# Output channels dealt over the SBUF partitions of a sparse 3x3 convolution, in a pattern of 16 x 8

## Chip, cores, metric

One core of one Trainium2 chip. The metric is device time in microseconds (us) of one execution. A page of the profile shows one profiled execution, whose span from first to last instruction is some 2 us shorter than the time. A run over 1.5% above the fastest of its kernel counts as slow, and ratios leave it out. "Row" below is one partition's contiguous piece of a DMA, here 16 KB of one output channel.

## The reference

```python
batch, c_in, h, w, c_out, k = 16, 64, 64, 64, 128, 3      # x: 16x64x64x64 f32, weight: 128x64x3x3 f32
x_pad = np.pad(x, ((0, 0), (0, 0), (1, 1), (1, 1)))
for b, co, ci, kh, kw:                                      # cut: five nested loops
    output[b, co] += weight[co, ci, kh, kw] * x_pad[b, ci, kh:kh+h, kw:kw+w]
```

x is 16.8 MB, the output 33.6 MB. The weights are 90% zeros, which the kernel does not use.

## The kernel before

Two images lie side by side on the 128 input partitions. TensorE makes the nine taps as matmuls; nearly everywhere it works on pairs of rows, whose input rows GpSimd has added up first. ScalarE (ACT) and VectorE (DVE) bring the sums from PSUM (the matmuls' output memory) to `o`, in SBUF (the on-chip memory that the DMA engines read): one tile of 128 channels x 64 x 64 per image, channel c on partition c. Stores of the first two pairs of images are held back until the loads are nearly done.

```python
    w_sb = const_pool.tile([C_OUT, C_IN * KH * KW], FP32, name="w_sb")
    nc.sync.dma_start(out=w_sb, in_=weight.rearrange("o i kh kw -> o (i kh kw)"))
    x_head = o_pool.tile([128, H, W], FP32, name="o")
    nc.sync.dma_start(out=x_head[:, 0:HEAD, :], in_=pair(0)[:, 0:HEAD, :])        # x's first half, cast later
    nc.gpsimd.dma_start(out=xs[0][:, HEAD:H, :], in_=pair(0)[:, HEAD:H, :])       # its second half, cast by the DMA
    ident = const_pool.tile([128, 128], BF16, name="ident")
    make_identity(nc, ident)
    for p in range(1, NP):
        nc.gpsimd.dma_start(out=xs[p], in_=pair(p))
    # ... cut: casts and transposes of the weights, matmuls, evictions ...
    HELD = 2
    held = []

    def store(p, n, o, a, b):
        return nc.sync.dma_start(out=out[2 * p + n][:, a:b, :], in_=o[n][:, a:b, :])

    for p in range(NP):
        o = [o_pool.tile([C_OUT, H, W], FP32, name="o") for _ in range(2)]
        # ... cut: four blocks of rows; at p == HELD, after the first block, the held stores go out,
        #     the first of them behind a wait for that block's last eviction ("loads first");
        #     the last pair is stored in two halves of rows, all others whole ...
```

Of the kernel before, what the change touches and what calls it, by code (L numbers as in the profile page):

```python
# [27 lines left out]
def kernel(  # L28
# [6 lines left out]
    nc = tc.nc  # L35
# [21 lines left out]

    xs = [x_pool.tile([128, H, W], BF16, name=f"x{p}") for p in range(NP)]
    w_sb = const_pool.tile([C_OUT, C_IN * KH * KW], FP32, name="w_sb")
    nc.sync.dma_start(out=w_sb, in_=weight.rearrange("o i kh kw -> o (i kh kw)"))  # L60
    x_head = o_pool.tile([128, H, W], FP32, name="o")
    nc.sync.dma_start(out=x_head[:, 0:HEAD, :], in_=pair(0)[:, 0:HEAD, :])
    nc.gpsimd.dma_start(out=xs[0][:, HEAD:H, :], in_=pair(0)[:, HEAD:H, :])  # L63
# [112 lines left out]
    held = []  # L176

    def store(p, n, o, a, b):
        return nc.sync.dma_start(out=out[2 * p + n][:, a:b, :], in_=o[n][:, a:b, :])

    for p in range(NP):
        o = [o_pool.tile([C_OUT, H, W], FP32, name="o") for _ in range(2)]
        last = p == NP - 1
        for blk in range(4):
            r0 = 16 * blk
            if BLOCKS[p][blk] == "T":
                done = twos(p, o, r0)
            else:
                for r, rows in ((r0, 8), (r0 + 8, 8)):
                    direct(p, o, r, rows)  # L190
            if last and blk % 2 == 1:
                for n in range(2):
                    store(p, n, o, r0 - 16, r0 + 16)
            if p == HELD and blk == 0:
                first = store(*held[0])
                tc.add_manual_dep(
                    first.ins,
                    done.ins.name,
                    mybir.DependencyInfo(
                        mybir.DependencyClass.Sync, mybir.DependencyReason.DATA  # L200
                    ),
                    reason="loads first",
                )
                for args in held[1:]:
                    store(*args)
        if p < HELD:
            held += [(p, n, o, 0, H) for n in range(2)]
        elif not last:
            for n in range(2):
                store(p, n, o, 0, H)  # L210
# [30 lines left out]
```

## Time and profile before

| | kernel before |
|---|---|
| time | 128.09 us (127.72 to 129.0, 4 runs beside the changed kernel) |
| span of the profiled run | 125.6 us |
| store of 2 MB, issue to landing, median | 17.0 us |
| 16 KB store row on its engine, mean (median) | 615 ns (611 ns) |

### The profile page before, as it was taken

To read this page: it belongs to the slowest core of one execution; us is meant where nothing else is said; L and a number is where in the kernel's file an instruction comes from. 1 tells how busy PE (TensorE), PEld (TensorE's weight loads), DVE (VectorE), ACT (ScalarE), POOL (GpSimd) and SP (SyncE) were. 2 spreads that over 40 slices of the span, in tenths; PEclk is the share of its full clock that TensorE was granted. 3 is DMA by queue.
4 is the path that set the end of the run, shared out by engine and by line. 5 is a ranking of instruction groups with operands and counts; after the bars stand their busy time and mean duration, and the time that the engine had idled before them with its cause. 6 is when DMAs were issued, how large, how long until landed. Compare 5 with 4: busy or idle time off the path is not lost.

```text
span 125.6 us, 2486 instructions
## 1 busy us (share of the span) xinstructions
PE 108.9 (87%) x1002; PEld 57.2 (46%) x1002; DVE 82.3 (66%) x135; ACT 38.9 (31%) x71; POOL 40.7 (32%) x45
## 2 busy tenths in 40 slices
PE   6669999999999999999999999999999999960000
PEld 6424455555555555545555555555555555420000
DVE  0352577877787778777877878887888787770000
ACT  4541533333333333333333333333333333320000
POOL 6937333333333333333333333333333310000000
PEclk9999999999999999999999999999999999999555
DMA  4999999999999999999999999999999999999960
GB/s 126 353 223 224 214 209 214 211 224 217 217 209 214 318 425 433 438 428 420 423 433 428 438 428 417 428 433 420 443 428 417 417 417 428 428 410 412 425 269 10
DMA packets 4044, 42.93 MB, mean 342 GB/s; under 512 B 448, under 2 KB 448, under 8 KB 704
## 3 DMA queue, kind: packets, MB, share of 16 engines
q1 hardware_dynamic: 2880, 34.90, 66.0%
q0 software_dynamic: 1152, 7.86, 30.2%
q8 instruction: 8, 0.13, 0.4%
q14 instruction: 4, 0.03, 0.1%
HBM read 17.07 MB, written 33.55 MB: 403 GB/s over the span
## 4 chain that ended last, share of the span: by engine, by line
PE 82%; DMA 4%; DVE 1%; issue 1%; DVEq 0%; SPq 0%
PE ps L135 82%; DMA o<-in_x_dram 4%; DVE o L168 1%; DVEq L236 0%; DVE x L87 0%; SPq L60 0%; DVEq L168 0%
## 5 line engine op out<-in xcount | busy, mean ns | idle before, releaser
L168 DVE TENSOR_TENSOR o<-ps,pc 128x512 f32<-128x512 f32 x124 | 77.8, 686 | 22.1 <-PE ps L135 19.8
L135 PE MATMUL ps<-x,wT 64*128 64x504 bf16 (+3 forms) x780 | 90.0, 377 | 1.8 <-DVE x L87 1.8
L135 PEld LDWEIGHTS <-wT 64*128 64x128 bf16 x966 | 53.6, 95 | 52.6 <-issue 3.3
L154 POOL TENSOR_TENSOR s<-x 128x512 bf16<-128x512 bf16 x31 | 35.6, 1152 | 59.3 <-PE ps L135 43.1
L161 ACT COPY pc<-ps 128x512 f32<-128x512 f32 x62 | 33.3, 589 | 64.0 <-issue 61.8
L135 PE MATMUL ps<-s,wT 64*128 64x512 bf16 (+1 forms) x186 | 25.6, 377 | 0.0
L74 PE MATMUL ps<-idle_rhs 128*128 128x128 bf16 x27 | 3.1, 313 | 1.0 <-DVE idle_rhs L71 1.0
L67 POOL DMA_DIRECT2D x<-in_x_dram x7 | 3.7, 561 | 0.0
L149 DVE COPY o<-ps 128x512 f32<-128x512 f32 x2 | 1.4, 692 | 3.3 <-PE ps L135 3.3
L74 PEld LDWEIGHTS <-idle_rhs 128*128 128x128 bf16 x27 | 2.8, 148 | 1.0 <-DVE idle_rhs L71 1.0
L91 DVE CAST w_bf<-w_sb 128x192 bf16<-128x192 f32 (+1 forms) x4 | 1.1, 349 | 2.8 <-DMA w_sb<-in_weight_dram 2.8
L148 ACT COPY o<-ps 128x512 f32<-128x512 f32 x2 | 1.2, 586 | 3.7 <-PE ps L135 3.7
L87 ACT CAST x<-o 128x576 bf16<-128x576 f32 (+1 forms) x2 | 1.5, 802 | 0.8 <-DMA o<-in_x_dram 0.8
L87 DVE CAST x<-o 128x576 bf16<-128x576 f32 x1 | 0.5, 461 | 1.9 <-DMA o<-in_x_dram 1.9
L91 ACT ACT_TABLE_LOAD x1 | 1.3, 1283 | 0.7 <-PEq L225 0.7
L97 PE MATMUL ps<-ident,w_bf 128*128 128x128 bf16 x9 | 1.2, 308 | 0.3 <-DVE w_bf L91 0.3
L91 ACT CAST w_bf<-w_sb 128x64 bf16<-128x64 f32 (+1 forms) x2 | 0.7, 416 | 1.7 <-DMA w_sb<-in_weight_dram 1.7
L97 PEld LDWEIGHTS <-w_bf 128*128 128x128 bf16 x9 | 0.8, 129 | 0.7 <-DVE w_bf L91 0.7
L101 DVE TENSOR_TENSOR wT<-ps,wT 128x384 bf16<-128x384 f32 x2 | 1.0, 548 | 0.0
L63 POOL DMA_DIRECT2D x<-in_x_dram x1 | 0.7, 696 | 0.8 <-POOLq L225 0.8
L71 DVE MEMSET idle_rhs<- 128x64 uint32 x1 | 0.1, 112 | 0.8 <-PEq L225 0.8
L110 ACT CAST wT<-ps 128x384 bf16<-128x384 f32 x1 | 0.5, 478 | 0.3 <-PE ps L97 0.3
(8 smaller groups left out, 1.9 us busy)
## 6 DMA issues: line engine op xcount, KB each, us to landing
out_dram<-o SPq DMA_DIRECT2D x14, 2048.0 KB, 17.0
x<-in_x_dram POOLq DMA_DIRECT2D x7, 1024.0 KB, 25.1
out_dram<-o SPq DMA_DIRECT2D x4, 1024.0 KB, 11.0
o<-in_x_dram SPq DMA_DIRECT2D x1, 1024.0 KB, 5.6
x<-in_x_dram POOLq DMA_DIRECT2D x1, 512.0 KB, 7.5
w_sb<-in_weight_dram SPq DMA_DIRECT2D x1, 288.0 KB, 3.0
```

Of the source, the lines that this page charges most:

```text
L67: nc.gpsimd.dma_start(out=xs[p], in_=pair(p))
L74: nc.tensor.matmul(idle_ps, idle_rhs, idle_rhs, start=True, stop=True)
L87: copy(out=xs[0][:, a:b, :], in_=x_head[:, a:b, :])
L91: copy(out=w_bf4[:, g, a:b, :], in_=w_v[:, k : k + b - a, :])
L97: nc.tensor.matmul(wps[:, j, :], src, ident, start=True, stop=True)
L101: nc.vector.tensor_tensor(out=wT[:, g], in0=wps, in1=wT[:, G1], op=SUB)
L135: nc.tensor.matmul(ps[n][:, lo:hi, c_lo:c_hi], tap(g, kw, n), src[q, a:b:step, c_lo + kw - 1 : c_hi + kw - 1], start=(i == 0), stop=(i == ...
L148: nc.scalar.copy(out=o[0][:, r0 : r0 + rows, :], in_=ps[0])
L149: nc.vector.tensor_copy(out=o[1][:, r0 : r0 + rows, :], in_=ps[1])
L154: nc.gpsimd.tensor_tensor(out=s, in0=xs[p][:, r0 : r0 + 16 : 2, :], in1=xs[p][:, r0 + 1 : r0 + 16 : 2, :], op=ADD)
L161: nc.scalar.copy(out=c, in_=shared[n])
L168: done = nc.vector.tensor_tensor(out=o[n][:, first : r0 + 16 : 2, :], in0=ps[n], in1=pc[n], op=ADD)
```

## The change

Its intent: what the 16 engines write at one moment should be sixteen neighbouring channels, 256 KB in one piece. Which channels an engine writes at which moment, no trace shows. Nothing in the computation changes; the weights are loaded in the same permuted order in which the channels are stored.

```diff
-    nc.sync.dma_start(out=w_sb, in_=weight.rearrange("o i kh kw -> o (i kh kw)"))
+    nc.sync.dma_start(
+        out=w_sb,
+        in_=weight.rearrange("(a b) i kh kw -> b a (i kh kw)", b=16),
+    )
...
     def store(p, n, o, a, b):
-        return nc.sync.dma_start(out=out[2 * p + n][:, a:b, :], in_=o[n][:, a:b, :])
+        dst = out[2 * p + n].rearrange("(a b) h w -> b a h w", b=16)
+        return nc.sync.dma_start(out=dst[:, :, a:b, :], in_=o[n][:, a:b, :])
```

## The prediction

The recorded text is cut, and the cuts are marked, where it told of the hardware what no run here shows. With them go terms of its sum: the cost of a clash in the stores (0 to +69 us, some 30 as a middle) and 0.7 us for the weight load. The sum came to 127.6 to 128.9 us without a clash and to 132 to 198 with one; the point was 134 us, and the range ended at 182. By a clash it means store rows up to twice as long as their floor of 611 ns, by a lead how far one engine is ahead of another.

> **What bounds the kernel now.** I read the page's row of slices first, then its queues, then the engines by stretches of time, then the chain that ended last with the list of DMA issues, and last the packet records and landings in the trace.
>
> ```profile
> PE   6669999999999999999999999999999999960000
> ...
> DMA  4999999999999999999999999999999999999960
> GB/s 126 353 223 224 214 209 214 211 224 217 217 209 214 318 425 433 438 428 420 423 433 428 438 428 417 428 433 420 443 428 417 417 417 428 428 410 412 425 269 10
> ...
> q1 hardware_dynamic: 2880, 34.90, 66.0%
> q0 software_dynamic: 1152, 7.86, 30.2%
> ...
> HBM read 17.07 MB, written 33.55 MB: 403 GB/s over the span
> ```
>
> Two rows are full: PE from the fourth slice to the 36th, DMA from the second to the 38th (a slice is 125.6/40 = 3.14 us). The GB/s row looks half empty up to slice 13, but there the loads cast to bf16 and the row counts the 7.86 MB they write, half of what they read. So the DMA engines have no slack in either half: x in the first, stores in the second.
>
> ```profile
> core 0: us, PE busy (x) PEld busy (x) DVE busy (x) ACT busy (x) POOL busy (x), PEclk, DMA share, GB/s
> ...
> 60.00:80.00 20.00, 20.00 (x192) 10.35 (x190) 15.93 (x27) 6.44 (x12) 6.91 (x6) 1.00 1.00 427
> 80.00:100.00 20.00, 20.00 (x190) 10.32 (x188) 15.79 (x27) 6.59 (x13) 6.97 (x7) 1.00 1.01 427
> 100.00:113.30 13.30, 11.94 (x112) 5.95 (x108) 10.53 (x17) 4.14 (x8) 1.10 (x1) 1.00 1.00 419
> 113.30:125.60 12.30, 0.00 (x0) 0.00 (x0) 0.00 (x1) 0.00 (x0) 0.00 (x0) 0.60 0.66 277
> ```
>
> PE and DMA are full side by side; after 113.3 us only DMA works.
>
> ```profile
> PE ps L135 82%; DMA o<-in_x_dram 4%; DVE o L168 1%; DVEq L236 0%; DVE x L87 0%; SPq L60 0%; DVEq L168 0%
> ...
> out_dram<-o SPq DMA_DIRECT2D x14, 2048.0 KB, 17.0
> ...
> out_dram<-o SPq DMA_DIRECT2D x4, 1024.0 KB, 11.0
> ```
>
> The chain names PE, but its shares add up to some 90%; the rest is the last stores, which it does not follow. A 2 MB store takes 17 us to land where its bytes at 427 GB/s need 4.9: it waits behind two or three others. The landings of the last store (two halves' worth issued at 113.3) come between 120.9 us on the first engine and 124.4 on the last. From 113.3 to 120.9 is 7.6 us of work, of which the last two 1 MB stores are 2.1 MB / 427 GB/s = 4.9; so 2.7 us of backlog were there when PE had finished. The store queue never ran dry: **the DMA rate sets the end**, and PE follows at most 2.7 us behind.
>
> The sum agrees. One engine's share is 8 rows of every transfer. A 16 KB store row takes 611 ns in 88% of the packet records (mean 617), a half row 313, a cast load row 625. Stores: 14 x 8 x 0.617 + 4 x 8 x 0.313 = 79.1 us. Loads: 7 x 8 x 0.625 + 16 x 0.313 + weights 0.8 = 40.8. With the first packet at 1.7 us that makes 121.6; the last packet ends at 124.0. The store rate, 16 x 16384 B / 611 ns = 429 GB/s, is a floor repeated to the nanosecond, not a mean over stalls.
>
> [...]
>
> **The change part by part.**
> - *Compute*: partition p holds channel 16(p mod 8) + p div 8 from the weight load to the store. Transposes, matmuls, evictions keep their shapes and counts. Cost 0.
> - *Packets*: each row stays one contiguous run (2304 B, 8 or 16 KB) on both sides. 20 hardware DMAs, the same 2560 data packets. Issue cost: 386 ns median on SP, maybe more for a pattern with one dimension more, but SP waits 99 us for DVE in total. Cost 0.
> - *HBM side*: [...] A better locality can save only what is above the floor: (617 - 611)/611 = 1% of 79 us = 0.8 us. It may do nothing.
> - *SBUF side*: [...] The leads: in the last x load, before the stores take over, nine of 16 engines landed within 0.43 us (0.7 of a row), the last 2.9 us later (4.7 rows); in the stores near the end the spread is 3.6 us. So leads are small at first and wander by single stalls (0.3 to 0.9 us). [...]
> - *Weight load*: [...]
>
> Sum: without a clash 128.4 - 0.8 to + 0.5 us; with one, some 132 to 198 us, middle near 160, since nothing hides a slower store.
>
> **The rivals.**
> 1. *Nothing changes* (about 128.4 us)[...]
> 2. [...]
> 3. *A better balance* (down to 126 us): the last engine lands 3.5 us after the first and 2.5 us after the mean of the 16 (121.9). If its lag came from the addresses it always writes, dealing the channels would spread it. Against: the lag is there in the x loads too (1 us, then 2.9) and grows in steps; between 15 and 113 us there are eight 16 KB instruction fetches beside it, which stay.
> 4. *PE becomes the bound*: only if stores sped up by over 2.7 us; they cannot at the floor.
>
> **Range and chances.** I give the clash a little over half (0.52)[...]. No visible change 0.42, a gain over 2% (2.6 us, the whole skew) 0.06. The mixture has its middle at about 134 us, between its two humps and itself not a favourite: under it lies all of rivals 1 and 3, above it the clash. The tenth part lies under 127.2 us[...].
>
> **What would show it.** The length of 16 KB store rows decides: 611 ns still in nine tenths of them means no clash; lengths up to 1222 ns, a GB/s row of 220 to 380 in the second half and a full PE row with gaps (DVE waiting for o buffers that are not yet stored) mean the clash. If rows stay at 611 and the end moves, the spread of the last landings must have moved with it. The weight load's 3.0 us to landing should grow by under 1 us. The prediction is wrong in its reasons if rows stay at 611 and the time still differs by over 2%, or if rows lengthen evenly on all engines [...].

## The result, and the profile after

The changed kernel takes 142.25 us (141.1 to 144.69, 4 runs, of which the longest counts as slow) against 128.09. The ratio is 1.106, 95% interval 1.094 to 1.118. Ratios here and below are the mean time of one kernel's fast runs over that of the other's in the same rounds, so not quite the ratio of the medians quoted. The span of the profiled run went from 125.6 to 139.2 us.

The rows by slices of the changed kernel (one slice is now 3.48 us):

```profile
PE   7309999999999999999949999999999999200000
...
DMA  4999999999996999999999999999999999999840
GB/s 99 287 273 221 219 217 212 214 219 212 214 219 129 226 257 264 287 306 351 377 409 414 414 433 424 424 421 428 428 428 409 438 414 419 381 318 377 341 181 28
```

But for the 13th slice, where loads give way to stores, DMA is as full as before. Yet from the 14th slice on it moves 226 to 287 GB/s where the kernel before soon moved 420. The rate then climbs for some 25 us, reaches the old 425, and falls again near the end. Busy engines at half the rate means rows that take longer. The engines by stretches of time say the same, one line of the kernel before and then three of the changed one:

```profile
41.00:60.00 19.00, 19.00 (x182) 9.73 (x179) 14.77 (x24) 6.44 (x12) 6.93 (x6) 1.00 1.01 413
```

```profile
core 0: us, PE busy (x) PEld busy (x) DVE busy (x) ACT busy (x) POOL busy (x), PEclk, DMA share, GB/s
...
41.00:60.00 19.00, 19.00 (x182) 9.46 (x178) 14.80 (x25) 6.45 (x12) 6.92 (x6) 1.00 0.93 232
60.00:80.00 20.00, 18.06 (x154) 8.77 (x152) 12.63 (x21) 5.37 (x10) 5.77 (x5) 0.91 1.00 384
80.00:100.00 20.00, 20.00 (x191) 10.55 (x189) 15.90 (x27) 6.45 (x12) 6.91 (x6) 1.00 1.01 426
```

Between 60 and 80 us PE, too, has a gap. The waits and the chain name it: DVE waits for `o` buffers that are not stored yet (before it had no such wait), and the chain now runs through a store.

```profile
DVE o L172 <- DMA out_dram<-o: 4.6, 2, 3.9
```

```profile
PE ps L139 57%; DMA out_dram<-o 17%; DMA o<-in_x_dram 6%; SPq L184 2%; DVE o L172 2%; SPq L61 0%; DVEq L241 0%; DVE x L91 0%; DVEq L172 0%
...
out_dram<-o SPq DMA_DIRECT2D x14, 2048.0 KB, 22.7
...
out_dram<-o SPq DMA_DIRECT2D x4, 1024.0 KB, 17.3
o<-in_x_dram SPq DMA_DIRECT2D x1, 1024.0 KB, 8.3
...
w_sb<-in_weight_dram SPq DMA_DIRECT2D x1, 288.0 KB, 3.6
```

The last two lines show a second thing: x's first half lands 8.3 us after its issue. In the kernel before they read:

```profile
o<-in_x_dram SPq DMA_DIRECT2D x1, 1024.0 KB, 5.6
...
w_sb<-in_weight_dram SPq DMA_DIRECT2D x1, 288.0 KB, 3.0
```

The start by time, SP's and GpSimd's issues and the first matmul on x, before:

```profile
0.74 0.38 SPq L60 DMA_DIRECT2D w_sb<-in_weight_dram  x1
...
1.17 0.43 SPq L62 DMA_DIRECT2D o<-in_x_dram  x1
1.24 0.70 POOL L63 DMA_DIRECT2D x<-in_x_dram  x1 [0.79 <-POOLq L225]
...
7.36 5.29 PE L135 MATMUL ps<-x,wT 64*128 64x512 bf16 x36 [1.83 <-DVE x L87]
```

and after:

```profile
0.74 0.66 SPq L61 DMA_DIRECT2D w_sb<-in_weight_dram  x1
...
1.24 0.70 POOL L67 DMA_DIRECT2D x<-in_x_dram  x1 [0.79 <-POOLq L230]
1.46 0.56 SPq L66 DMA_DIRECT2D o<-in_x_dram  x1
...
10.34 5.74 PE L139 MATMUL ps<-x,wT 64*128 64x512 bf16 x36 [4.47 <-DVE x L91]
```

The weight load with its extra dimension takes 0.66 instead of 0.38 us to issue, so the load of x's first half is issued after GpSimd's load of the second half, not before. In the packet records the consequence is plain. Between 4.5 and 5.0 us the engines of the kernel before start 26 rows of the first half and none of the second. Those of the changed kernel start 12 of the first and 14 of the second. The half that is needed first shares the engines with the one that is needed later, and the first matmul on x starts 3.0 us later.

From the packet records, the mean length of the 16 KB store rows that start in stretches of 8 us (without the eight instruction fetches of the same size, which the prediction's row mean of 617 ns includes; all these tables come from one profiled run of each kernel):

| ns | 43-51 us | 51-59 | 59-67 | 67-75 | all |
|---|---|---|---|---|---|
| before | 617 | 615 | 614 | 615 | 615 |
| after | 1138 | 971 | 768 | 651 | 697 |

And from the landings of each store on the 16 engines, the time between the first engine's and the last engine's, for the first five stores in order: changed kernel 1.3, 3.2, 5.3, 6.6, 7.0 us; it stays between 7.0 and 7.5 up to the 13th. Before: 2.5, 2.5, 2.5, 2.3, 2.3.

The records carry no engine numbers, but on a busy engine a row starts within some 20 ns of the end of the one before it, so the rows can be strung into chains, one for each engine, with some doubt where two ends coincide. In the changed kernel 31 of the 32 rows that are second and third in the 16 chains take 1204 to 1406 ns. Soon many chains repeat every four rows, as one does with 611, 611, 864, 1496, 611, 611, 613, 1496 ns. Of the rows over 900 ns that start between 50 and 66 us, 64% are followed by another such row four rows later, and 21% two rows later (43% of all rows there are so long).

Now the 13.6 us between the spans (the last landing moved from 124.5 to 138.1) can be put together, per engine in the mean of the 16: whole store rows 112 x (697 - 615) ns = 9.2 us, half rows 32 x (345 - 313) ns = 1.0 us, the later start 2.0 us (not measured by itself, but what is left of the 12.2 us by which the mean landing of the last store moved; the first store row starts 2.4 us later, at 44.3 us), and 1.5 us because the last engine now lands 4.1 us after the mean, before 2.6.

### The profile page after: what moved, and what is told of

Same layout as the page of the kernel before. It is cut to its first block, busy times and chain, and to the rows that moved or that the text cites. A ratio compares the mean times of both kernels' runs of the same rounds, so it can differ in the third digit from the quotient of the medians.

```text
span 139.2 us, 2486 instructions
## 1 busy us (share of the span) xinstructions
PE 110.9 (80%) x1002; PEld 57.2 (41%) x1002; DVE 82.2 (59%) x135; ACT 39.0 (28%) x71; POOL 40.8 (29%) x45
## 4 chain that ended last, share of the span: by engine, by line
PE 57%; DMA 23%; SPq 3%; DVE 2%; issue 1%; DVEq 0%
PE ps L139 57%; DMA out_dram<-o 17%; DMA o<-in_x_dram 6%; SPq L184 2%; DVE o L172 2%; SPq L61 0%; DVEq L241 0%; DVE x L91 0%; DVEq L172 0%
## 5 line engine op out<-in xcount | busy, mean ns | idle before, releaser
L139 PE MATMUL ps<-x,wT 64*128 64x504 bf16 (+3 forms) x780 | 94.5, 382 | 6.4 <-DVE x L91 4.5
L139 PE MATMUL ps<-s,wT 64*128 64x512 bf16 (+1 forms) x186 | 28.9, 385 | 0.0
L116 DVE CAST wT<-ps 128x384 bf16<-128x384 f32 x1 | 0.6, 551 | 0.0
```

Source lines behind the costliest of these rows:

```text
L139: nc.tensor.matmul(ps[n][:, lo:hi, c_lo:c_hi], tap(g, kw, n), src[q, a:b:step, c_lo + kw - 1 : c_hi + kw - 1], start=(i == 0), stop=(i == ...
```

## The experiments

**The theories.** P: how a store's 128 partitions are cut up, here into 16 x 8, is what costs, at whatever addresses; while the engines go in step, two of them at a time hold each other up, and rows take up to twice as long (the clash). That it is two is the estimate, from rows of 1138 ns beside 617; what they might share, no trace shows. H: HBM takes the new addresses more slowly. S: the later start is what costs. D: the longer access pattern is slower in itself. Later L: the leads of engines over one another grow as long as the store queue is never empty, which ends the clash. The runs were made in four groups, each on one chip with the kernel before beside it, so ratios compare better than times. Eight of the kernels below give a wrong channel order or mixed images, as is said; all compute the same sums, and only those with a lead and their control move more bytes. The 95% intervals are in brackets.

### Only the stores dealt

Edit, against the changed kernel: the weight load back as it was. The order is wrong.

> The weight load as before, only the stores dealt (the output channels come out permuted, wrong on purpose). Theory P [...]: the 16 KB store rows of the first 8 us of stores take 1000 to 1200 ns as in the changed kernel, the first matmul on x starts at 7.4 us as in the kernel before, and the time is 136 to 141 us. Rival S (the later start of x and with it of the first store makes the 14 us): rows stay at 611 ns and the time is under 130 us.

Measured: 138.24 us median (135.64 to 139.89, 4 runs). Only one of them counts as fast (the others lie over 1.5% above it), so there is no verdict with an interval. Store rows in the four stretches: 788, 786, 655, 623 ns. First matmul on x at 7.2 us. S alone falls: with the start as before, rows are long and most of the loss is there. The early rows are shorter than the 1000 to 1200 ns expected. This part of the expectation is missed, and why this run has less of the clash is not shown; its profile is that of the fastest of the four runs.

### Two rows of 64 channels

```diff
-        dst = out[2 * p + n].rearrange("(a b) h w -> b a h w", b=16)
+        dst = out[2 * p + n].rearrange("(a b) h w -> b a h w", b=64)
```
(weights as before; order wrong)

> Weights as before; stores dealt in two rows of 64 channels ([...] order wrong on purpose). Theory P: [...] the early rows take 1000 to 1200 ns and the time is within 2% of the stores-dealt run. Rival H [...] the rows are near 611 ns and the time is under 131 us.

Measured: 127.81 us, ratio 1.002 [0.998, 1.006]; rows 617, 615, 614, 615 ns. P as I had put it is missed: this pattern too has an extra dimension and no plain order of channels, and it costs nothing. D falls for this pattern. Either HBM addresses were the cause after all, or 64 in the slowest dimension does not do what 16 does. The next three runs decide that.

### 16 x 8 with neighbouring channels

```diff
-        dst = out[2 * p + n].rearrange("(a b) h w -> b a h w", b=16)
+        both = out[2 * p : 2 * p + 2].rearrange("n c h w -> (n c) h w")
+        dst = both.rearrange("(b m a) h w -> m b a h w", m=2, a=8)[n]
```
(weights as before; the channels of two images are mixed)

> Weights as before. Stores with 16 x 8 on the DRAM side[...] (the two images' channels are mixed, wrong on purpose). Theory P [...]: early rows over 1000 ns in a good part, time 134 to 141 us as with the dealt stores. Theory H [...]: rows at 611, time under 130 us.

Measured: 138.11 us, 1.083 [1.076, 1.090]; rows 985, 903, 702, 634 ns. Its GB/s row:

```profile
GB/s 152 323 224 212 217 215 212 222 215 212 215 217 292 287 241 280 294 328 369 396 410 410 425 420 444 420 417 429 429 425 405 434 439 408 364 321 393 330 169 24
```

The same dip and climb as in the changed kernel, though each index of the slowest dimension now holds eight neighbouring channels, a run of 128 KB. H falls: what the changed kernel has in common with this one is 16 x 8, not the addresses.

### The dealing with 32 in place of 16

```diff
-        in_=weight.rearrange("(a b) i kh kw -> b a (i kh kw)", b=16),
+        in_=weight.rearrange("(a b) i kh kw -> b a (i kh kw)", b=32),
...
-        dst = out[2 * p + n].rearrange("(a b) h w -> b a h w", b=16)
+        dst = out[2 * p + n].rearrange("(a b) h w -> b a h w", b=32)
```
(results right)

> The change with 32 in place of 16 in both patterns, results right: channels dealt, neighbouring ones still 16 KB apart, but the slowest dimension 32 as with the harmless 64. Theory P [...]: rows at 611 ns, time 127 to 130 us. Theory H: rows over 1000 ns at first as in the changed kernel, time 135 us or more.

Measured: 132.85 us, 1.037 [1.031, 1.043]; rows 631, 619, 624, 617 ns. Its rows are as expected, its time is not: 127 to 130 us were expected. The missing 3 us are in the start. The first matmul on x is at 12.3 us, and the first store is issued at 45.9 us, when all loads have landed (44.5 us) and the engines stand idle:

```profile
DMA  3999999999999059999999999999999979999990
```

That is mended in the section "The start mended" below.

### Each store in two halves of the partitions

```diff
-        return nc.sync.dma_start(out=out[2 * p + n][:, a:b, :], in_=o[n][:, a:b, :])
+        first = None
+        for c in (0, 64):
+            d = nc.sync.dma_start(
+                out=out[2 * p + n][c : c + 64, a:b, :], in_=o[n][c : c + 64, a:b, :]
+            )
+            first = first or d
+        return first
```
(against the kernel before; results right)

> The kernel before with each store cut in two, partitions 0-63 and 64-127: same channels to the same addresses, no dealing. Theory P: [...] rows of over 1000 ns appear until some engines lead, time over 132 us. Theory H: rows at 611, time within 2% of before.

Measured: 140.16 us, 1.094 [1.087, 1.100]; rows 1144, 917, 720, 638 ns.

```profile
GB/s 152 318 221 223 214 214 221 211 216 218 211 218 207 254 223 285 299 337 358 385 413 423 423 423 437 401 418 451 399 432 437 404 425 415 356 306 349 339 188 17
```

Every channel goes to the address it had in the kernel before, nothing is dealt, no pattern has an extra dimension, and the same loss appears, dip and climb included. Together with the last two runs this leaves P's core: neither addresses nor the pattern's dimensions explain the loss, and what the slow kernels share is how a store's 128 partitions are cut up, 16 x 8 or two of 64. The rhythm of the rows is much the same too: here 62% of the rows over 900 ns have another four rows later and 26% two rows later (starts from 48 to 64 us); with 16 x 8 and neighbouring channels it is 51% and 24%. Which partitions an engine reads stands in no trace, so why such a cut costs, and why long rows come back every four, is not shown.

### Only the weights dealt

Edit, against the kernel before: the weight load of the change, stores untouched. The order is wrong.

> Only the weight load dealt, stores as before (channel order wrong on purpose). The changed kernel's weight load takes 0.66 instead of 0.38 us to issue, x's first half then no longer goes ahead of its second half and lands 3 us later. Theory W (that matters): first matmul on x at 10.3 us instead of 7.4, first store 3 us later, and as up to 2.7 us of PE's lag are hidden under the store backlog, the time is 128 to 131 us. If W is without weight, under 128.5 us. Store rows stay at 611 ns either way.

Measured: 130.03 us, 1.017 [1.014, 1.020], so 2.2 us. First matmul on x at 10.1 us, first store at 43.6 us (before 39.7). Rows 632, 618, 625, 619 ns. As expected: the late first half of x is a cost of its own. It reaches the end because the DMA engines are partly idle for a moment at the change-over from loads to stores (the 5 below), where the kernel before has no such gap:

```profile
DMA  2999999999999599999999999999999979999990
```

### The start mended, with 32 and with 16

The same edit to the dealing with 32 and to the changed kernel: the load of x's second half moves behind the identity matrix and a memset, so it cannot get ahead of the first (it is issued at 2.14 us, the first half at 1.46).

```diff
-    nc.gpsimd.dma_start(out=xs[0][:, HEAD:H, :], in_=pair(0)[:, HEAD:H, :])
     ident = const_pool.tile([128, 128], BF16, name="ident")
     make_identity(nc, ident)
+    pad = const_pool.tile([128, 1024], FP32, name="pad")
+    nc.gpsimd.memset(pad, 0.0)
+    nc.gpsimd.dma_start(out=xs[0][:, HEAD:H, :], in_=pair(0)[:, HEAD:H, :])
```

> The 32 x 4 dealing of weights and stores (results right), and the load of x's second half issued behind the identity matrix and a 1 us memset, so that it can no longer get ahead of x's first half. Theory: the 4 to 5 us of the previous 32 x 4 run were the late first half of x alone, so the first matmul on x comes back to 7.4 to 8.5 us, the store rows stay at 611 ns, and the time is that of the kernel before, 127 to 129 us: dealing in itself is worth nothing. If the start is not the cause, 131 us or more.

Measured: 128.01 us, 1.003 [0.997, 1.009], results right; rows 617, 615, 614, 616 ns. The first matmul on x, by time:

```profile
7.30 5.38 PE L141 MATMUL ps<-x,wT 64*128 64x512 bf16 x36 [1.44 <-DVE x L93]
```

So the dealing of channels, in a form that keeps the rows at 611 ns and with the start mended, is worth nothing here: neighbouring channels, 16 KB apart, side by side in the pattern neither helped nor hurt.

> The changed kernel itself with the same mended start (results right). [...] 135 to 140 us, some 2 to 5 us under the changed kernel, early store rows of 1000 ns and more in a good part.

Measured: 138.76 us, 1.089 [1.081, 1.096], results right; rows 1021, 886, 722, 632 ns. The start is worth some 1.7% here too (1.106 to 1.089, though the two come from different chips and their intervals just touch); the other 8.9% stay with the 16.

### A lead set by hand

If engines lose because they go in step, a lead should end it at once. Edit, against "only the stores dealt": two loads of x into a scratch tile ahead of the first store, of 4 x 8 and 12 x 8 rows, meant to send some engines into the stores some rows behind others. (Their landing semaphores show 5 and 13 updates, that of the one load of the run called "wrong pairs" 9, and that of the control's load of 128 partitions 16. Which engines took part in each, no trace shows.)

```diff
+    lead = const_pool.tile([128, 2048], FP32, name="lead")
...
-                first = store(*held[0])
+                first = nc.sync.dma_start(out=lead[0:32],
+                    in_=x[0:4, 0:8, 0:32, :].rearrange("a b h w -> a b (h w)"))
...  # first still waits for the block's last eviction
+                nc.sync.dma_start(out=lead[32:128],
+                    in_=x[0:12, 8:16, 0:32, :].rearrange("a b h w -> a b (h w)"))
-                for args in held[1:]:
+                for args in held:
```
The control has one load of 128 partitions (`lead` whole, `x[0:16, 0:8, 0:32, :]`). The wrong pairs have one load of 64 (`lead[0:64]`, `x[0:8, 0:8, 0:32, :]`); their name comes from the guess at which engines hold each other up, which no trace shows.

> Stores dealt as in the first run, and just ahead of the first store two extra loads [...]. Theory P: [...] store rows average under 650 ns from the start, and the time is 4 to 8 us under that of the stores-dealt run although 1 MB is added (2.4 us in the mean[...]): 130 to 135 us. Rivals H (HBM addresses) and D [...]: rows as in the stores-dealt run, time 2 to 5 us above it.

> Control for the lead: the same 1 MB of extra loads, four row times on every engine, so no lead. All theories: early rows of 1000 to 1200 ns as in the stores-dealt run and a time 2 to 3 us above it.

> Weights as before, stores dealt, and one extra load [...]. Theory P [...]: no help, a share of rows over 1000 ns in the first 16 us of stores like that of the control without a lead, time 136 to 140 us. If any stagger helps (a burst of 16 engines at once is what costs), rows and time as in the run with the lead, 133 to 135 us.

> The kernel with the four-row lead [...] once more, beside the wrong pairs on one chip: mean store row 630 to 640 ns, first 16 us of stores under 650 ns, time 2 us or more under that of the wrong pairs.

> The four-row lead [...], five rounds. If the lead pays in time as well as in rows: 1 to 5 us under the control of the next run. If not, the later clash at the end takes it back and the two are within 1%.

> The control with the same bytes and no lead, five rounds: 138 to 140 us as in its first run; store rows of the first 16 us of stores 650 to 800 ns in the mean.

| run | rows, first three stretches, ns | first matmul on x in the profiled run | time, us | ratio |
|---|---|---|---|---|
| lead | 643, 622, 624 | 7.2 us | 136.43 (133.06 to 141.24) | 1.050 [1.041, 1.060] |
| lead again | (9 rows), 705, 696 | 12.0 | 138.73 | 1.083 [1.073, 1.092] |
| lead, five rounds | (12 rows), 719, 674 | 11.8 | 139.17 | 1.085 [1.081, 1.089] |
| no lead | 654, 798, 683 | 7.4 | 138.59 | 1.086 [1.082, 1.089] |
| no lead, five rounds | 673, 802, 700 | 7.5 | 139.06 | 1.089 [1.085, 1.094] |
| wrong pairs | 935, 847, 700 | 7.4 | 139.01 | 1.080 [1.071, 1.089] |

In the rows the first lead run does what was expected: stores of the first 16 us are near the floor. But its control is as short in the first stretch (654 ns, where 1000 to 1200 were expected) and differs only in the second, where it has near 800. The two other lead profiles have 705 and 696, 719 and 674 ns (of "lead again" under 650 was expected, a miss). Both are of runs that count as slow (143.05 and 141.14 us), with stores that start some 7 us later, so they are not weighed against the control. The load of the wrong pairs leaves rows of 935 and 847 ns, so the shape of what goes ahead seems to matter; why is not shown. It is one profile, and that load moves half the bytes of the lead.

In the time the gain did not repeat: in the first group lead and control had 1.050 and 1.086 (two fast runs with the lead), with five rounds 1.085 and 1.089, and beside the wrong pairs 1.083 against 1.080, where 2 us were expected. Two things blur it. What the two loads of the lead cost in themselves is not measured, and in the two slow profiles one engine got its share of x's first half 5 us late, for a reason I have not found; those runs start at 12 us. That a lead would pay in time is therefore not shown.

### One store at a time

What ends the clash? If leads grow while the queue has work, taking the backlog away should keep the clash for good. Edit, to the stores dealt and, as a control, to the kernel before: each store waits for the landing of the one before it.

```diff
+        d = nc.sync.dma_start(...)
+        if landed:
+            tc.add_manual_dep(d.ins, landed[-1].ins.name, mybir.DependencyInfo(
+                mybir.DependencyClass.Sync, mybir.DependencyReason.DATA), reason="one store at a time")
+        landed.append(d)
+        return d
```

> Weights as before, dealt 16 x 8 stores, and each store waits until the one before has landed (order wrong on purpose). Theory L: every store starts with all engines in step, so no lead is carried over, rows of 1000 ns and more persist from the first store to the last (mean 1000 to 1200 ns), each 2 MB store takes 9 to 11 us from issue to landing instead of 6 to 7, and the time is 180 to 215 us. If the early clash comes from the change-over from loads to stores alone, only the first stores are slow and the time is within 10 us of the serialised control.

> Control: the kernel before with each store waiting for the landing of the one before. Rows at 611 ns, 6 to 7 us from issue to landing of a 2 MB store, time 140 to 160 us.

Measured: 229.5 us (1.796 [1.786, 1.806]) against 153.83 us for the control (1.206 [1.200, 1.212]), beyond even the 215 us expected. Rows: 1124 ns in the mean, median 1226, and no shorter in the last whole stores (1134 ns) than in the second (1135); the control 621 ns. Rate and landing, dealt and one at a time:

```profile
GB/s 241 225 211 216 219 213 213 274 197 185 190 139 232 139 235 139 229 142 232 143 211 159 208 165 206 159 211 143 232 136 235 125 243 125 246 122 164 162 162 161
...
out_dram<-o SPq DMA_DIRECT2D x14, 2048.0 KB, 11.3
```

and the control:

```profile
GB/s 175 296 223 213 220 213 218 209 218 220 216 397 172 345 213 414 276 414 224 332 349 278 410 254 371 310 246 414 278 410 134 427 272 280 414 239 257 263 263 220
...
out_dram<-o SPq DMA_DIRECT2D x14, 2048.0 KB, 6.4
```

A 2 MB store takes 11.3 - 6.4 = 4.9 us more, which is 8 x 0.611 us, as much as a full doubling for the engine that lands last. Over all engines the rows take 1124/621 = 1.81 times as long: one row in seven stays under 700 ns even here. The rate never climbs. The landings of each whole store spread over 1.2 to 2.0 us only, where the changed kernel's reach 7. This agrees with theory L: without a backlog the clash never ends and costs 49% (229.5 over 153.83), with one the engines drift apart and it costs 8.9%. The drift is seen over all 16 landings; which engine leads which is not seen.

## Why the prediction was right and wrong

- **What bounds the kernel: right.** The DMA rate sets the end. Rows that took 9.2 + 1.0 us longer per engine moved the mean landing, and the 2.0 us left over agree with the 2.2 us that the later start cost alone. Three readings were loose without harm. The backlog of 2.7 us is that of the first engine to finish; by the last engine's landing it was 11.1 - 4.9 = 6.2. Twelve, not nine, of the engines landed within 0.43 us in the last load of x. And the packets of the weights add up to 1.1 us an engine, not 0.8.
- **Compute, packet count, HBM side: right.** HBM was given 0 to -0.8 us; dealing with 32 measured 1.003.
- **SBUF side: that it costs was right, why it does is not shown.** Rows of 611 ns became 1138 ns in the first 8 us, 1.86 times and within the 1222 ns, twice the floor, that the prediction named. 16 x 8 is slow with both sets of addresses that were tried (1.089 with the start mended, and 1.083), 64 x 2 (1.002) and, once the start is mended, 32 x 4 (1.003) are not. How the prediction came to expect this of 16 is cut: no trace gives an engine's number, or shows anything that two engines share. Carried over to 64 x 2, the same argument failed (rows of 617 ns where 1000 to 1200 were expected).
- **Its size: wrong, and this is the step that failed.** The clash term was put at some 30 us as a middle because leads "are small at first and wander by single stalls". It measured 10.2 us. The leads did not wander: they grew from store to store, 1.3 to 7.0 us of spread within five stores, and the clash was gone after some 25 us. It came back in part near the end (664 ns in the rows of 115 to 123 us), where the last pair's stores of half rows begin; why is not shown. Where no backlog lets leads grow, rows stay near double (1124 against 621 ns) and the time is 229.5 against 153.8 us.
- **The weight load: wrong in its way.** It was given +0.7 us by a clash of its own. That clash did not show: its rows took 140 ns in the mean, before 139, though their pattern is 16 x 8 too, and why is open. Its landing grew by 0.6 us (3.0 to 3.6), of which 0.44 are a later first packet. But its issue was 0.28 us longer, which swapped the order of two loads of x: 2.2 us, measured alone as 1.017.
- **The spread at the end** (1.5 us more between mean and last engine) was not in the sum. It fits the same leads: the spread of the last store went from 3.5 to 8.1 us.
- **The number.** 134 us was, as it said, a middle between two humps and no favourite. A clash was given "132 to 198 us, middle near 160"; 142 lies in that, in its lower part. Hedging between the humps put the point at +6 us where +14 came: it came out too low although the clash term was too high, and that it is no further off is luck. Issue cost on SP was put at 0 with "maybe more"; the issue of a store went from 386 to 1332 ns in the median (least 332 and 537), and no wait shows that it mattered there.

What stays open: why leads grow under a backlog instead of staying put (1.3 to 7.0 us within five stores), why 82 of the 1792 rows took over 1250 ns, many near 1500 and one 2153, longer than twice the floor, 1222 ns, why 16 x 8 makes rows long, why 32 and 64 keep the rows short, and what a preset lead is worth in time.

## What to carry to other kernels

A rearranged pattern on the DRAM side of a DMA can change how fast its rows move although no row changes: 1138 ns in place of 617 at the start here, for a reason that is not shown. Check with one run that the row length stays where it was: here, in the first 8 us of stores, it did with 128, 64 and 32 in the slowest dimension (617, 617, 631 ns), and did not with 16 and with two stores of 64 partitions (1138, 1144). A transfer at its floor (here the same 611 ns in 88% of its records) leaves little to gain from better addresses, and here they gained nothing (1.003). And when two loads on different queues compete, a quarter of a microsecond of issue time can decide which goes first, as it did here (0.28 us, which cost 2.2).
